# A decoder step on one Trainium2 core: the sample group's recurrence as wide vector work, a narrower weight load, and the closing halves swapped

## The chip, the core and the metric

The kernel runs on one core of a Trainium2 chip. TensorE multiplies matrices (its weight loads are listed apart, as PEld), VectorE (DVE) and ScalarE (ACT) work on 128 partitions side by side, GpSimd (POOL) makes masks and issues some transfers, and SyncE (SP) issues nearly all DMA transfers. Each engine works through its own queue in order and waits on semaphores. Matmuls write to PSUM, the accumulator memory; everything else lives in SBUF. The metric is the device time of one execution in microseconds; lower is better.

## The reference, cut to what matters

One inference step of a two-layer decoder serves a prompt of 1024 tokens and a sample group of 8 single tokens with the same weights. Layer 0 mixes tokens with a gated linear recurrence (4 heads, a 128 x 128 state per head) beside attention into a memory; layer 1 uses stick-breaking attention. Each layer ends in a SwiGLU feed-forward block. All is float32.

```
def step(S, inp):                      # recurrence, chunk by chunk
    b = jnp.cumsum(fi, axis=2)
    o_inter = jnp.einsum('bhtk,bhkv->bhtv', qi * jnp.exp(b), S)
    att = jnp.einsum('bhtk,bhsk,bhtsk->bhts', qi, ki, dec)
    o = o_inter + jnp.einsum('bhts,bhsv->bhtv', att, vi)
    S_new = jnp.exp(b_last[:, :, 0, :, None]) * S + jnp.einsum(
        'bhsk,bhsv->bhkv', ki * jnp.exp(b_last - b), vi)
    return S_new, o
h = h + rmsnorm(mix, g[1])
h = h + rmsnorm(swiglu(rmsnorm(h, g[2]), w_gu[l], w_down[l]), g[3])
```

For a sample there is one token, so the recurrence is one update: with the forget factor f, key k, value v and query q of a head (vectors of 128), the state becomes S = f * S + k v^T (f and k along the rows), and the output is q^T S. There are 8 samples x 4 heads = 32 such states, 2 MB in all; they are read, updated, and written back as an output.

## The kernel before

**Tiles.** Activations lie with features on partitions and tokens along the free dimension. The prompt is cut into two groups of 512 tokens; group 1 carries the 8 samples as columns 512 to 519 (`G : G + NB`). A float32 operand is split into a float32r high part (a cast on ScalarE) and a low part (a subtraction on VectorE, `split_to`), and products are made of three float32r matmuls. Plain float32 matmuls appear in the trace as two records each. Weights come in tiles of 128 x 512 (`split_w`, lines 201 to 207): a load on SyncE's queue, a cast, a subtraction, then 12 or 24 matmuls on line 220.

**The order of the work.** Each part of the program is a generator. `weave` advances several of them in turn, in proportion to given weights, each up to its next `yield`; this gives the program order. A planner then lays out every engine's queue when the kernel is built: among the instructions that its model of times says are ready, the one earliest in program order goes first. On the chip each queue then runs in that order, whatever the real times are. Buffers come from pools with a fixed number of slots: 4 of the 128 x 1024 kind (`C`), 7 of 128 x 512 (`B`), 3 PSUM banks for small products (`S`).

**The sample group's recurrence** (`hgrn_sample`, lines 1088 to 1145) is woven with the output gate's projection, a part of group 0's feed-forward block and the forming of weight sums:

```
weave((a1.sample(), 6), (a1.gate(), 4), (f0.part(1), 9), (w0, 9))
```

Keys and values of the 8 samples are transposed to 8 rows (lines 1096, 1097). Per head, the 8 states are loaded as a 128 x 1024 tile (line 1110), each 128 columns one sample. VectorE places each sample's value row at its own 128 columns of an 8 x 1024 tile with zeros elsewhere (line 1113, the constant `bdm`), and multiplies the state by the forget factors (line 1117). Two matmuls with 8 rows of weights form the outer products k v^T (line 1122), which VectorE adds to the state (line 1123). For the output, queries are spread into a 128 x 8 x 8 selector form (line 1105), so that eight matmuls of 128 x 8 weights (line 1125) put each sample's q^T S on its own row of `po`. The state is stored (line 1128). After the four heads, `po` is copied out (line 1131), transposed back to feature columns (line 1134), normalised, and written over the sample columns of the tile `Ft`, from which `merge` (line 1264) later takes it.

The same selector constant exists in float32r as `selr` and is used by `sample_pv` (line 948): weights of 128 x 8 that are all ones in one column sum the 128 partitions of a product onto one row. `sample_scores` (lines 914 to 937) sends 8 rows through a small DRAM tensor and reads them back on all 128 partitions.

**The prompt's recurrence** (`hgrn_prompt`, lines 1147 to 1223) builds the 128 x 128 block of attention weights of each chunk in seven levels of doubling block size m = 1 to 64. At each level a matmul of all 128 keys of a chunk (the weights) with the 64 queries of the upper half-blocks (line 1174) gives products, of which a predicated copy on VectorE (line 1184) takes those that a mask allows. At the top level, m = 64, the allowed ones are exactly those of the first 64 keys.

**The closing rows** (`ffn_w.close`, lines 664 to 695, and `out_rows`, lines 741 to 793). The last part of the last feed-forward block of group 1 works on one half of the columns after the other: 256 prompt columns first, then 256 prompt columns and the 8 samples (264). The first pass also loads and splits the weights. Each half ends with transposes to token rows (line 753), sums of squares by matmuls against a column of ones (line 768), two ScalarE operations for the norm, two VectorE operations per block of rows (lines 782 and 785) and a store per block: two blocks in the first half, three in the second (the samples being the third).

Of the kernel before, what the change touches and what calls it, by code (L numbers as in the profile page):

```python
# [18 lines left out]
P = 128  # L19
# [4 lines left out]
def tile_decoder(  # L24
# [550 lines left out]
    class ffn_w:  # L575
# [88 lines left out]
        def close(self, f0, nf, mids):  # L664

            l = self.l
            ws = []
            for a in range(2):
                d = slice(2 * P * a, (2 * P, NG[1])[a])
                h = d.stop - d.start  # L670
                acc = small([P, h], tag="st", bufs=3)
                rows = out_rows(self, a)
                for m in range(ND):
                    if a == 0:
                        ws.append(split_w(w_down[l], f0, nf, m * P, self.spl4))
# [9 lines left out]
                    nc.vector.tensor_add(R, R, ps[:, :h])  # L685
# [400 lines left out]
            yield  # L1086

    def hgrn_sample(Ft, Kt, Qt, vs):
        HB = H * NB
        kc = small([P, HB], tag="ss")  # L1090
        for h in range(H):
            nc.vector.tensor_copy(kc[:, h * NB : (h + 1) * NB], Kt[h // 2][:, h % 2, G : G + NB])
        pk = S()
        pvv = S()
        for h in range(H):
            nc.tensor.transpose(pk[:NB, h * P : (h + 1) * P], kc[:, h * NB : (h + 1) * NB], ident)
            nc.tensor.transpose(pvv[:NB, h * P : (h + 1) * P], vs[:, h, :], ident)
        kT = B()
        nc.vector.tensor_copy(kT[:NB, :512], pk[:NB, :])
        vT = B()  # L1100
        nc.vector.tensor_copy(vT[:NB, :512], pvv[:NB, :])
        po = S()
        for h in range(H):
            qd = small([P, NB, NB], tag="qd", bufs=2)
            nc.vector.tensor_mul(
                qd, sel, Qt[h // 2][:, h % 2, G : G + NB].unsqueeze(2).to_broadcast([P, NB, NB])
            )
# [5 lines left out]
            nc.vector.tensor_mul(  # L1113
                vbv[:NB], vT[:NB, h * P : (h + 1) * P].unsqueeze(1).to_broadcast([NB, NB, P]),
                bdm.to_broadcast([NB, NB, P]),
            )
            nc.vector.tensor_mul(
                stv, stv, Ft[h // 2][:, h % 2, G : G + NB].unsqueeze(2).to_broadcast([P, NB, P])
            )
            for a in range(2):  # L1120
                ps = S()
                nc.tensor.matmul(ps, kT[:NB, h * P : (h + 1) * P], vb[:NB, a, :], start=True, stop=True)
                nc.vector.tensor_add(st[:, a, :], st[:, a, :], ps)
            for b in range(NB):
                nc.tensor.matmul(
                    po[:NB, h * P : (h + 1) * P], qd[:, b, :], stv[:, b, :], start=(b == 0), stop=(b == NB - 1)
                )
            nc.sync.dma_start(st_sample[0, :, h].rearrange("b k v -> k b v"), stv)
            yield
        ot = B()  # L1130
        nc.vector.tensor_copy(ot[:NB, :], po[:NB, :])
        pr = S()
        for h in range(H):
            nc.tensor.transpose(pr[:, h * NB : (h + 1) * NB], ot[:NB, h * P : (h + 1) * P], ident[:NB, :NB])
# [12 lines left out]
    def hgrn_prompt(g, Ft, Kt, Qt, Vt):  # L1147
# [15 lines left out]
        for lv in range(7):  # L1163
            m = 1 << lv
            nbg = G // (2 * m)
            for hp in range(2):
# [3 lines left out]
                for hh in range(2):  # L1170
                    for c in range(CH):
                        cs = slice(c * P, (c + 1) * P)
                        rhs = Q_[:, hh, cs].rearrange("p (b t m) -> p b t m", t=2, m=m)[:, :, 1, :]
                        nc.tensor.matmul(plv[:, hh, c, :], K_[:, hh, cs], rhs, start=True, stop=True)  # L1174
                for hh in range(2):
                    Qv = Q_[:, hh, :G].rearrange("p (b t m) -> p b t m", t=2, m=m)
                    Kv = K_[:, hh, :G].rearrange("p (b t m) -> p b t m", t=2, m=m)
# [282 lines left out]
    with tc.issue_after(made[0].ins):  # L1460
# [47 lines left out]
        for blk in range(2):  # L1508
# [11 lines left out]
        nc.gpsimd.affine_select(  # L1520
            bdm.rearrange("p b o -> p (b o)"), ones[:NB, :NB], pattern=[[-1, NB]], compare_op=ALU.is_equal,
            fill=0.0, base=0, channel_multiplier=1,
        )
    drain(head)
    a0 = mixer_a(0, x0)
    drain(a0.v(), a0.fq())
# [100 lines left out]
```

## Time and profile before

| what | us |
|---|---|
| median of 3 runs | 2471.2 |
| lowest and highest of the 3 runs | 2469.78, 2472.68 |
| the profiled execution's own time | 2472.22 |
| its span, first to last instruction of the program | 2470.5 |
| largest group: matmuls of line 220 on normed inputs, 6240 records | 1119.5 busy |
| line 1174, 448 matmul records | 53.2 busy |
| mean traffic of the DMA engines | 160 GB/s |

How to read the lines that follow: the page has one row per group of instructions, with line number in the kernel, engine, operation, tile written <- tiles read, shapes, count, busy time, mean of one in ns, then the idle time of the engine just before and what ended it. The busy time of TensorE is of pipelined matmuls whose durations overlap, so the cost of one in a dense run is better read from the chain of waits, where a piece is start, duration, what, and the number of instructions in it. The chain follows the work that ended last back to its releasers, so that a piece of it is time that set the end. Stretches are given from the start of the span.

### The profile page before, as it was taken

To read this page: it belongs to the slowest core of one execution; us is meant where nothing else is said; L and a number is where in the kernel's file an instruction comes from. 1 tells how busy PE (TensorE), PEld (TensorE's weight loads), DVE (VectorE), ACT (ScalarE), POOL (GpSimd) and SP (SyncE) were. 2 spreads that over 40 slices of the span, in tenths; PEclk is the share of its full clock that TensorE was granted. 3 is DMA by queue.
4 is the path that set the end of the run, shared out by engine and by line. 5 is a ranking of instruction groups with operands and counts; after the bars stand their busy time and mean duration, and the time that the engine had idled before them with its cause. 6 is when DMAs were issued, how large, how long until landed. Compare 5 with 4: busy or idle time off the path is not lost.

```text
span 2470.5 us, 42287 instructions
## 1 busy us (share of the span) xinstructions
PE 2436.5 (99%) x15971; PEld 2176.6 (88%) x15971; DVE 1639.5 (66%) x2988; ACT 1236.6 (50%) x2377; POOL 184.2 (7%) x316
## 2 busy tenths in 40 slices
PE   8999999999999999999999999999999999999998
PEld 6888888877879998899999989877777888999998
DVE  5767556754788685655756685778688466755666
ACT  5437544243445554555444554555554445664445
POOL 1000101100000000111200101212000100000000
PEclk9999999999999999999999999999999999999999
DMA  6354666546745437767666649754253573465542
GB/s 188 116 167 111 156 192 160 127 134 164 212 150 154 140 120 227 201 163 183 162 196 174 193 128 274 228 150 146 91 177 117 138 199 120 139 187 145 152 143 74
DMA packets 530503, 395.29 MB, mean 160 GB/s; under 512 B 21237, under 2 KB 468802, under 8 KB 530298
## 3 DMA queue, kind: packets, MB, share of 16 engines
q1 hardware_dynamic: 501114, 312.88, 42.4%
q0 software_dynamic: 29184, 79.70, 14.0%
q8 instruction: 126, 2.06, 0.3%
q14 instruction: 79, 0.65, 0.1%
HBM read 362.69 MB, written 101.11 MB: 188 GB/s over the span
## 4 chain that ended last, share of the span: by engine, by line
PE 88%; DVE 5%; DMA 3%; issue 2%; ACT 2%; POOL 0%; SPq 0%; DVEq 0%; ACTq 0%; POOLq 0%
PE mm L220 47%; PE q L511 13%; PE q L648 9%; PE q L464 3%; PE s L1174 2%; PE mm L1042 2%; PE s L906 1%; DMA c<-in_cache_mem_v 1%; PE s L1370 1%; PE mm L824 1%; PE mm L851 1%; PE q L680 1%; PE s L875 1%; PE s L1336 1%; PE s L899 1%
## 5 line engine op out<-in xcount | busy, mean ns | idle before, releaser
L220 PE MATMUL mm<-x,ws 128*128 128x260 f32 (+1 forms) x6240 | 1119.5, 335 | 3.2 <-DVE r L657 1.7
L220 PEld LDWEIGHTS mm<-x,ws 128*128 128x128 f32 x6240 | 941.6, 188 | 127.3 <-issue 2.7
L206 ACT CAST ws<-w 128x512 fp32r<-128x512 f32 (+1 forms) x652 | 382.8, 588 | 548.9 <-PE mm L220 396.9
L207 DVE TENSOR_TENSOR ws<-w,ws 128x512 fp32r<-128x512 f32 (+1 forms) x652 | 419.2, 648 | 253.5 <-ACT ws L206 243.5
L220 PE MATMUL mm<-m,ws 128*128 128x512 f32 (+1 forms) x1344 | 280.3, 360 | 0.5 <-DVE r L400 0.5
L220 PEld LDWEIGHTS mm<-m,ws 128*128 128x128 f32 x1344 | 218.0, 188 | 37.2 <-issue 1.0
L648 PE MATMUL q<-m,ws 128*128 128x260 f32 (+1 forms) x1824 | 221.7, 282 | 0.0
L648 PEld LDWEIGHTS q<-m,ws 128*128 128x128 f32 x1824 | 218.9, 188 | 1.1 <-DVE t L534 0.3
L502 DVE TENSOR_TENSOR ws<-w,ws 128x512 fp32r<-128x512 f32 x181 | 123.9, 690 | 87.6 <-ACT ws L501 86.1
L501 ACT CAST ws<-w 128x512 fp32r<-128x512 f32 x181 | 111.8, 621 | 109.2 <-PE q L648 32.5
L511 PE MATMUL q<-x,ws 128*128 128x260 f32 (+1 forms) x1188 | 158.1, 282 | 0.0
L511 PEld LDWEIGHTS q<-x,ws 128*128 128x128 f32 x1188 | 148.6, 188 | 0.0
L511 PE MATMUL q<-y,ws 128*128 128x260 f32 x912 | 119.9, 283 | 0.4 <-ACT q L521 0.2
L511 PEld LDWEIGHTS q<-y,ws 128*128 128x128 f32 x912 | 113.7, 189 | 1.1 <-ACT q L518 0.6
L464 PE MATMUL q<-x,ws 128*128 128x260 f32 (+1 forms) x720 | 91.3, 284 | 0.3 <-DVE r L400 0.2
L464 PEld LDWEIGHTS q<-x,ws 128*128 128x128 f32 x720 | 88.4, 188 | 1.8 <-DVE r L400 0.5
L511 PE MATMUL q<-a,ws 128*128 128x260 f32 (+1 forms) x672 | 87.1, 282 | 0.0
L511 PEld LDWEIGHTS q<-a,ws 128*128 128x128 f32 x672 | 83.2, 188 | 0.0
L657 DVE TENSOR_TENSOR r<-r,q 128x260 f32<-128x260 f32 (+1 forms) x128 | 48.4, 420 | 48.8 <-PE q L648 48.8
L237 DVE TENSOR_SCALAR t<-mm 128x512 f32<-128x512 f32 (+1 forms) x58 | 40.1, 691 | 54.1 <-PE mm L220 53.8
L563 POOL COPY mk<-a 128x1 f32<-128x1 f32 x36 | 21.0, 583 | 645.6 <-ACT a L1226 393.9
L228 DVE TENSOR_TENSOR m<-t,m 128x512 fp32r<-128x512 f32 (+1 forms) x88 | 60.8, 691 | 9.5 <-ACT m L227 8.7
(358 smaller groups left out, 3038.2 us busy)
## 6 DMA issues: line engine op xcount, KB each, us to landing
w<-in_w_gu SPq DMA_DIRECT2D x297, 256.0 KB, 3.4
w<-in_w_down SPq DMA_DIRECT2D x160, 256.0 KB, 2.8
wsum<-in_w_gu POOLq DMA_DIRECT2D x72, 512.0 KB, 6.5
w<-wsum SPq DMA_DIRECT2D x104, 256.0 KB, 3.5
w<-in_w_in_a SPq DMA_DIRECT2D x80, 256.0 KB, 3.3
w<-in_w_o SPq DMA_DIRECT2D x64, 256.0 KB, 2.8
wsum<-in_w_gu POOLq DMA_DIRECT2D x24, 640.0 KB, 7.0
wsum<-wsum POOLq DMA_DIRECT2D x24, 512.0 KB, 5.8
```

Of the source, the lines that this page charges most:

```text
L206: nc.scalar.copy(ws[:, 0, :n, :], raw[:, :n, :])
L207: nc.vector.tensor_sub(ws[:, 1, :n, :], raw[:, :n, :], ws[:, 0, :n, :].bitcast(F32))
L220: nc.tensor.matmul(ps[:, a, : PW[g]], wt, xt[k][:, xi, o : o + PW[g]], start=(k == 0 and wi == 0), stop=(k == nk - 1 and wi == 2),)
L228: nc.vector.tensor_sub(dst[1], src, dst[0].bitcast(F32))
L464: ins = nc.tensor.matmul(pp[a][:, :h], wt, xt[k][:, xi, a * h : (a + 1) * h], start=(k == 0 and wi == 0), stop=(k == ND - 1 and wi == 2),)
L501: nc.scalar.copy(w[:, 0, :], src)
L502: nc.vector.tensor_sub(w[:, 1, :], src, w[:, 0, :].bitcast(F32))
L511: nc.tensor.matmul(ps[:, :h], w[:, wj, k * P : (k + 1) * P], x[:, xi, :], start=(first and k == 0 and wi == 0), stop=(k == 3 and wi == 2), ...
L648: nc.tensor.matmul(pp[a][:, :h], wt, mids[k][:, xi, a * h : (a + 1) * h], start=(k == 0 and wi == 0), stop=(k == nf - 1 and wi == 2),)
L657: nc.vector.tensor_add(d, d, pp[a][:, :h])
L1042: nc.tensor.matmul(pb[i][:, a, :], xt[k][:, xi, c * P : (c + 1) * P], ws[:, s, :], start=(k == 0 and wi == 0), stop=(k == ND - 1 and wi == 2),
L1174: nc.tensor.matmul(plv[:, hh, c, :], K_[:, hh, cs], rhs, start=True, stop=True)
```

## The change

Three edits.

1. In `hgrn_sample` the outer products and the output sums leave TensorE. The values of the 8 samples are written as 8 rows to a DRAM tensor (`vd`), and per head read back broadcast on all 128 partitions as a 128 x 1024 tile, as wide as the states. VectorE then makes f * S, k * v, their sum and q * S, each one operation of 1024 elements per partition. The last product is split in two float32r parts per half (512 columns, four samples), and matmuls with `selr` sum the partitions: row 2 h + a of `po` receives half a of head h, with four samples side by side. At the end the 8 rows go through a second DRAM tensor (`od`) to be regrouped from (head, half) rows to sample rows. There is one more `yield`, after the values' write. The key transposes, the selector form of the queries, and the constant `bdm` go.
2. In `close` the half with the samples comes first, and the weights are loaded with it.
3. In `hgrn_prompt`, at the top level, the matmul takes the first 64 keys alone as weights, and a plain copy on ScalarE of 64 partitions takes the place of the predicated copy.

```
-            for a in range(2):
+            for a in (1, 0):
...
-                    if a == 0:
+                    if a:
                         ws.append(split_w(w_down[l], f0, nf, m * P, self.spl4))
...
     def hgrn_sample(Ft, Kt, Qt, vs):
-        HB = H * NB
-        kc = small([P, HB], tag="ss")
-        for h in range(H):
-            nc.vector.tensor_copy(kc[:, h * NB : (h + 1) * NB], Kt[h // 2][:, h % 2, G : G + NB])
-        pk = S()
         pvv = S()
         for h in range(H):
-            nc.tensor.transpose(pk[:NB, h * P : (h + 1) * P], kc[:, h * NB : (h + 1) * NB], ident)
             nc.tensor.transpose(pvv[:NB, h * P : (h + 1) * P], vs[:, h, :], ident)
-        kT = B()
-        nc.vector.tensor_copy(kT[:NB, :512], pk[:NB, :])
         vT = B()
         nc.vector.tensor_copy(vT[:NB, :512], pvv[:NB, :])
+        vd = tc.dram_tile([NB, 512], F32, name=nm("vd"))
+        nc.sync.dma_start(vd, vT[:NB, :])
+        yield
...
         po = S()
         for h in range(H):
-            qd = small([P, NB, NB], tag="qd", bufs=2)
-            nc.vector.tensor_mul(
-                qd, sel, Qt[h // 2][:, h % 2, G : G + NB].unsqueeze(2).to_broadcast([P, NB, NB])
-            )
+            def col(t):
+                return t[h // 2][:, h % 2, G : G + NB].unsqueeze(2).to_broadcast([P, NB, P])
...
             nc.sync.dma_start(stv, state_hgrn[0, :, h].rearrange("b k v -> k b v"))
             vb = C()
             vbv = vb.rearrange("p a (b v) -> p (a b) v", v=P)
-            nc.vector.tensor_mul(
-                vbv[:NB], vT[:NB, h * P : (h + 1) * P].unsqueeze(1).to_broadcast([NB, NB, P]),
-                bdm.to_broadcast([NB, NB, P]),
-            )
-            nc.vector.tensor_mul(
-                stv, stv, Ft[h // 2][:, h % 2, G : G + NB].unsqueeze(2).to_broadcast([P, NB, P])
-            )
+            nc.sync.dma_start(vbv, vd[:, h * P : (h + 1) * P].partition_broadcast(P))
+            nc.vector.tensor_mul(stv, stv, col(Ft))
+            nc.vector.tensor_mul(vbv, vbv, col(Kt))
+            nc.vector.tensor_add(st, st, vb)
+            nc.sync.dma_start(st_sample[0, :, h].rearrange("b k v -> k b v"), stv)
+            nc.vector.tensor_mul(vbv, stv, col(Qt))
             for a in range(2):
-                ps = S()
-                nc.tensor.matmul(ps, kT[:NB, h * P : (h + 1) * P], vb[:NB, a, :], start=True, stop=True)
-                nc.vector.tensor_add(st[:, a, :], st[:, a, :], ps)
-            for b in range(NB):
-                nc.tensor.matmul(
-                    po[:NB, h * P : (h + 1) * P], qd[:, b, :], stv[:, b, :], start=(b == 0), stop=(b == NB - 1)
-                )
-            nc.sync.dma_start(st_sample[0, :, h].rearrange("b k v -> k b v"), stv)
-            yield
+                qs = B(F32R), B(F32R)
+                split_to(qs, vb[:, a, :])
+                for i, p in enumerate(qs):
+                    nc.tensor.matmul(
+                        po[:NB, :], selr[:, 2 * h + a, :], p,
+                        start=(h == 0 and a == 0 and i == 0), stop=(h == H - 1 and a == 1 and i == 1),
+                    )
+            yield
+        rows = B()
+        nc.vector.tensor_copy(rows[:NB, :], po[:NB, :])
+        od = tc.dram_tile([H, NB, P], F32, name=nm("od"))
+        nc.sync.dma_start(od.rearrange("h (a b) v -> (h a) b v", a=2), rows[:NB, :].rearrange("p (b v) -> p b v", v=P))
         ot = B()
-        nc.vector.tensor_copy(ot[:NB, :], po[:NB, :])
+        nc.sync.dma_start(ot[:NB, :].rearrange("p (h v) -> p h v", v=P), od.rearrange("h b v -> b h v"))
...
-                        nc.tensor.matmul(plv[:, hh, c, :], K_[:, hh, cs], rhs, start=True, stop=True)
+                        k = m if nbg == CH else P
+                        nc.tensor.matmul(
+                            plv[:k, hh, c, :], K_[:, hh, c * P : c * P + k], rhs, start=True, stop=True
+                        )
...
+                    if nb == 1:
+                        nc.scalar.copy(
+                            atts[hp * 2 + hh].rearrange("p (c t m) -> p c t m", c=CH, t=2)[:m, :, 1, :],
+                            plv[:m, hh, :, :],
+                        )
+                        continue
                     nc.vector.copy_predicated(
...
-        bdm = const.tile([NB, NB, 1], F32, name="bdm")
```

More of the change, by code (lines that the diff above doesn't have):

```diff
@@ L1088, in hgrn_sample @@
     def hgrn_sample(Ft, Kt, Qt, vs):
-        HB = H * NB
-        kc = small([P, HB], tag="ss")
-        for h in range(H):
-            nc.vector.tensor_copy(kc[:, h * NB : (h + 1) * NB], Kt[h // 2][:, h % 2, G : G + NB])
-        pk = S()
         pvv = S()
         for h in range(H):
-            nc.tensor.transpose(pk[:NB, h * P : (h + 1) * P], kc[:, h * NB : (h + 1) * NB], ident)
             nc.tensor.transpose(pvv[:NB, h * P : (h + 1) * P], vs[:, h, :], ident)
-        kT = B()
-        nc.vector.tensor_copy(kT[:NB, :512], pk[:NB, :])
         vT = B()
         nc.vector.tensor_copy(vT[:NB, :512], pvv[:NB, :])
+        vd = tc.dram_tile([NB, 512], F32, name=nm("vd"))
+        nc.sync.dma_start(vd, vT[:NB, :])
+        yield
+        HB = H * NB
+        assert 2 * H == NB
         po = S()
         for h in range(H):
-            qd = small([P, NB, NB], tag="qd", bufs=2)
-            nc.vector.tensor_mul(
-                qd, sel, Qt[h // 2][:, h % 2, G : G + NB].unsqueeze(2).to_broadcast([P, NB, NB])
-            )
+            def col(t):
+                return t[h // 2][:, h % 2, G : G + NB].unsqueeze(2).to_broadcast([P, NB, P])
             st = C()
@@ L1517, in tile_decoder @@
         nc.gpsimd.tensor_tensor(pidx, pidx, iot, op=ALU.add)
-        bdm = const.tile([NB, NB, 1], F32, name="bdm")
[L1520 to L1523, printed above, removed]
     drain(head)
```

## The prediction

> **What bounds the kernel now.** I read the page's busy shares first, then the chain of waits, then the chain and the timeline around the sample group's recurrence.
>
> ```profile
> span 2470.5 us, 42287 instructions
> PE 2436.5 (99%) x15971; PEld 2176.6 (88%) x15971; DVE 1639.5 (66%) x2988; ACT 1236.6 (50%) x2377; POOL 184.2 (7%) x316
> PE 88%; DVE 5%; DMA 3%; issue 2%; ACT 2%; POOL 0%; SPq 0%; DVEq 0%; ACTq 0%; POOLq 0%
> ```
>
> TensorE is busy 99% of the span and makes 88% of the chain that ends last. VectorE and ScalarE have slack on average. So the first question for each edit is how many microseconds of TensorE it removes in a stretch where TensorE has no gap, and the second whether it makes TensorE's queue wait.
>
> The edit's main place is the recurrence of the sample group. The chain between 480 and 640 us, in order of time (start, duration, what, count of matmul records), with its shares by line first:
>
> ```profile
> by line: PE mm L220 76.0%; PE s L1125 5.3%; PE s L1122 4.8%; PE s L1174 3.3%; PE s L1201 2.5%; PE s L1213 2.3%; PE s L1209 2.2%; PE s L256 1.9%; PE s L1195 1.1%; PE s L1096 0.3%; PE s L1097 0.3%; PE s L1134 0.2%; issue 0.0%
> 484.12 5.30 PE s L1174 x48
> ...
> 524.81 0.44 PE s L1096 x4
> ...
> 530.29 1.91 PE s L1122 x4
> ...
> 532.63 1.73 PE s L1125 x8
> 534.36 1.94 PE mm L220 x4
> 536.30 0.97 PE s L1125 x8
> 537.27 17.09 PE mm L220 x73
> 554.36 1.91 PE s L1122 x4
> ...
> 575.65 1.91 PE s L1122 x4
> ...
> 578.23 1.84 PE s L1125 x16
> ...
> 607.10 12.04 PE mm L220 x71
> ```
>
> The chain is TensorE from end to end: nothing but matmuls, back to back. Whatever leaves this queue here shortens the chain one for one, as long as nothing else takes its place. The recurrence's own shares are 4.8% of 160 us for line 1122 (four pieces of 1.91, 7.6 us), 5.3% for line 1125 (8.4 us) and 0.44 us for the key transposes of line 1096.
>
> The next rows are busy times by stretch (PE, weight loads, VectorE, ScalarE, GpSimd, then granted clock, DMA share, GB/s).
>
> ```profile
> 532.60:536.10 3.50, 3.50 (x13) 2.01 (x12) 2.32 (x3) 0.00 (x0) 0.00 (x0) 0.51 0.82 229
> sum 116.00, PE 115.98 PEld 89.67 DVE 66.67 ACT 46.30 POOL 8.09; mean PE 23.20 PEld 17.93 DVE 13.33 ACT 9.26 POOL 1.62
> ```
>
> The sum covers 524 to 640: TensorE 115.98 of 116 us, VectorE only 66.67, ScalarE 46.30. In the first row the clock is granted at 0.51 although TensorE is busy for all 3.50 us, right behind the first eight-row matmuls.
>
> **The change, part by part.** *Sample recurrence, TensorE.* It loses lines 1096, 1122 and 1125: 0.44 + 7.6 + 8.4 = 16.5 us. It gains 16 selector matmuls (4 heads, 2 halves, 2 split parts) of 8-column weights against 512 float32r columns. A 512-column record costs 17.09 / 73 = 0.234 us in the chain, so 16 cost 3.7 us; the same form exists on line 948, whose waits are small, and I add 0.3 us for such waits:
>
> ```profile
> L948 PE MATMUL ns<-b,selr 128*8 128x512 f32 x48 | 19.5, 434 | 0.8 <-DVE b L228 0.5
> L1174 PEld LDWEIGHTS s<-a,a 128*128 128x128 f32 x448 | 53.4, 192 | 1.2
> L1125 PEld LDWEIGHTS s<-c,qd 128*8 128x8 f32 x64 | 5.4, 93 | 3.5 <-issue 1.9
> ```
>
> Net -12.5 us. The value transposes (line 1097) and the output transposes (line 1134) stay.
>
> *The half clock.* The four line-220 records at 534.36 took 1.94 us where 4 x 0.234 = 0.94 would do. The dip follows matmuls that use 8 of 128 rows; they go, and -1.0 us with them. Line 948's 8-column form, which comes instead, ran at full clock (the row for 720 to 740, under rival B). Bounds: 0 if the dip comes from something else, -1.0 if not; I take -1.0, because it stands in this very stretch. The Trainium skill (TensorE: Matmul & The Clock Gate, What's actually happening) halves the clock after an idle window of about 3.4 us. This trace differs on the cause: TensorE was busy for all of those 3.50 us; by the page the dip would have nothing to do with these shapes and the sum would be 1.0 us less of a gain.
>
> *VectorE and ScalarE in that stage.* Rows of 524 to 640 (mean ns second from the bar):
>
> ```profile
> L207 DVE TENSOR_TENSOR ws<-w,ws 128x512 fp32r<-128x512 f32 x30 | 20.6, 688 | 8.4 <-ACT ws L206 8.4
> L1123 DVE TENSOR_TENSOR c<-c,s 128x512 f32<-128x512 f32 x8 | 5.4, 680 | 0.2 <-PE s L1122 0.2
> L1113 DVE TENSOR_TENSOR c<-b,bdm 8x1024 f32<-8x1024 f32 x4 | 4.8, 1210 | 0.6 <-DMA out_st_sample<-c 0.6
> L1117 DVE TENSOR_TENSOR c<-c,a 128x1024 f32<-128x1024 f32 x3 | 3.6, 1217 | 1.9 <-DMA c<-in_state_hgrn 1.9
> L1105 DVE TENSOR_TENSOR qd<-sel,a 128x64 f32<-128x64 f32 x2 | 0.4, 224 | 4.4 <-PE s L1125 4.4
> ACT ws L206 <- PE mm L220: 61.0, 26, 8.1
> ```
>
> Per head VectorE loses 0.22 + 1.21 + 2 x 0.68 = 2.8 us and gains three 1024-wide operations (key, add, query) and two split subtractions: 3 x 1.21 + 2 x 0.69 = 5.0 us. Over four heads that is +8.9 us, less one 0.68 us copy of the keys and four short ones. VectorE would be busy about 75 of 103 us; the cover is its idle time, so I cost it at 0. If that cover were gone it would cost up to 8.9 us. ScalarE gains eight casts of about 0.6 us, on 46.30 of 116. The last row (waits in this stage) is why: weights wait for TensorE, 61.0 us over 26 times, not TensorE for weights.
>
> *SyncE's queue and the loads.* It gains seven issues: the values' write, four broadcast loads, the outputs' write and read-back. Each broadcast moves 512 KB in 512-byte pieces, like the state's load. The nearest rows (DMA issues with us to landing; then SyncE's issues in time):
>
> ```profile
> c<-in_state_hgrn SPq DMA_DIRECT2D x4, 512.0 KB, 5.4
> b<-qd SPq DMA_DIRECT2D x24, 256.0 KB, 3.7
> out_y_prompt<-yT SPq DMA_DIRECT2D x4, 512.0 KB, 2.6
> 577.60 1.03 SPq L965 DMA_DIRECT2D c<-in_cache_mem_k  x1
> ...
> 611.87 0.37 SPq L965 DMA_DIRECT2D c<-in_cache_mem_k  x1
> 648.39 0.30 SPq L926 DMA_DIRECT2D qd<-b  x1
> 650.11 2.10 SPq L932 DMA_DIRECT2D b<-qd  x4
> ```
>
> A write to DRAM and the load that reads it are 1.7 us apart (648.39 to 650.11): that long SyncE stands once for the values and once for the outputs, with the weight loads behind it. Weights run ahead of TensorE here, so 0. The broadcasts land after about 5.4 us. Heads are about 20 us apart on TensorE (530.29, 554.36, 575.65), because the other matmuls of the weave are first in order, so the loads are covered: 0 of a possible 5.4 us per head.
>
> *The outputs' trip through DRAM.* Between the last selector matmul and line 1134's transposes there are now a write (1.7 us) and a read (below 3.7 us). Those transposes stand in TensorE's in-order queue; line 220's matmuls behind them wait if the data is late. Before, where only a copy stood between, 12.04 us of line-220 matmuls were laid there (607.10). Bounds: 0 and 5.4 us; I take +0.5. Everything behind (the norm, the gate's product) has its consumer a stage later.
>
> *One more pause.* The recurrence now yields once more ahead of its first head, so each head stands one step of the weave later, and with it the release of its two large buffers; the four memory-key loads at 577.60 to 611.87, which reuse them, move by up to 20 us. Their first use is after 650.11, and the last would land near 637: covered, 0.
>
> *The top level's 64 key columns.* 48 records of line 1174 take 5.30 us, 110 ns each, while the moving side has only 64 columns: the weight load paces them. A load of 128 columns shows 192 ns, one of 8 columns 93, so 0.83 ns per column, and 64 columns fewer save 53 ns. The level has 448 / 7 = 64 records. Bounds: 0 if 64 columns load no faster, 53 ns or 3.4 us at best. Where the load no longer paces, the moving side does: line 1125's records with 128 moving columns take 0.97 / 8 = 121 ns, so 64 may need some 60, which is 50 ns saved. I take that, the nearer end: -3.2 us. Eight predicated copies move from VectorE to plain copies on ScalarE; both have room, 0.
>
> *The closing order.* The work is the same; only the half behind the last matmul differs. Timeline of before, half 0 and then half 1:
>
> ```profile
> 2445.79 0.42 DVE L685 TENSOR_TENSOR r<-r,q 128x256 f32<-128x256 f32 x1
> ...
> 2450.47 0.74 DVE L785 SCALAR_TENSOR_TENSOR yT<-s,rr,hT 128x512 f32<-128x512 f32 x1
> 2459.83 1.47 PE L753 MATMUL s<-ident,r 128*128 128x128 f32 x12
> 2460.03 0.43 DVE L685 TENSOR_TENSOR r<-r,q 128x264 f32<-128x264 f32 x1
> 2466.45 0.73 DVE L785 SCALAR_TENSOR_TENSOR yT<-s,rr,c 8x512 f32<-8x512 f32 x1
> ```
>
> From the last addition to the last output operation half 0 takes 2451.21 - 2445.79 = 5.4 us, half 1 7.15: -1.7. But half 1's extra eight transposes (about 0.11 us each: 12 in 1.47) and four short sums now stand before the last matmul, about +1.2, and the store that lands last is 512 KB in place of 32 KB, perhaps +0.5. Sum 0, bounds -1.7 and +1.7.
>
> Sum: -12.5 - 1.0 + 0.5 - 3.2 + 0 = -16.2 us. The profiled execution took 2472.2 us (span 2470.5), 1.0 above the median of 2471.2; so 2456.0 there and 2455 for the median. A difference under 0.2% (4.9 us) is about what runs of this kernel cannot tell from none.
>
> **The rivals.** *A, full gain*: 2455. For it: no gap in TensorE over 116 us. Its own range is 2451 to 2461 (the top level saves nothing: +3.2; the trip costs 3 more; the tail's 1.7 each way).
>
> *B, the gain meets a full VectorE.* Later buffers push the sample group's memory attention, and with it VectorE work, into the stretch where VectorE has no room:
>
> ```profile
> 720.00:740.00 20.00, 19.21 (x110) 15.09 (x109) 18.68 (x33) 8.84 (x22) 0.00 (x0) 1.00 0.60 183
> sum 60.00, PE 58.50 PEld 48.14 DVE 54.82 ACT 31.62 POOL 0.76; mean PE 19.50 PEld 16.05 DVE 18.27 ACT 10.54 POOL 0.25
> ```
>
> From 700 to 760 VectorE works 54.82 of 60 us and TensorE already misses 1.5. About 8 us of added VectorE work there would be given back: 2463. Against it: the new work belongs 60 us earlier.
>
> *C, the trip stops TensorE.* If nothing is laid between, it stands 1.7 + 3.7 = 5.4 us, and a half-clock stretch like that of 532.60 costs 1.75 more: 7.2 in place of 0.5, 2462. Against: the 12 us laid between before. The Trainium skill (TensorE: Matmul & The Clock Gate, Why this matters for your kernels) warns of gaps over about 3 us between bursts of matmuls and so speaks for the second part; no such gap stands in the rows above.
>
> *D, the time was not TensorE's*: what supplies it sets the pace, and it idles for what it saved; 2471. Against: the 61.0 us of ScalarE waiting for TensorE.
>
> *E, slower: the heads' first selector matmul waits for its broadcast.* TensorE runs in order, so a late load stops it whole. At the full 5.4 us landing for each of four heads it loses 21.6 against a gain of 16.2: 2477. It decides from 16.2 / 4 = 4.05 us per head on. For: line 1117 once waited 1.9 us for a state. Against: 20 us between heads.
>
> **How the numbers follow.** A 0.62, B 0.13, C 0.08, D 0.06, E 0.11. Prediction: A's 2455. A, B and C are faster: 0.83; D is the same, 0.06; E slower, 0.11. The range runs over A, B and C: from 2449 (both best bounds and some luck in the order) to 2468.
>
> **What would show it.** Right: chain pieces of the recurrence of about 0.23 us per selector record and no lines 1122 and 1125; no clock of 0.5 near 535; level-six records at 60 ns; transposes of the outputs without a wait of TensorE ahead of them; TensorE's busy time lower by some 15 us. Wrong: a wait of TensorE on VectorE's split or on a broadcast at the selector matmuls (E), on the read-back (C), more than 1.5 us of TensorE gaps in the memory-attention stretch (B), or an order laid out anew that loses elsewhere.

## The result and the profile after

The changed kernel takes 2456.18 us in the median of four runs (2454.92 to 2457.05), the kernel before 2471.94 beside it (four runs, 2469.78 to 2473.18). The ratio is 0.9937, with an interval of 0.9920 to 0.9954. The profiled execution of the changed kernel took 2454.92 us, that of before 2472.22.

The page of the changed kernel (span, busy times by engine, shares of the chain):

```profile
span 2453.2 us, 42169 instructions
PE 2419.1 (99%) x15903; PEld 2167.8 (88%) x15903; DVE 1642.2 (67%) x2979; ACT 1241.7 (51%) x2393; POOL 184.3 (8%) x315
PE 88%; DVE 5%; DMA 3%; ACT 2%; issue 2%; POOL 0%; SPq 0%; DVEq 0%; ACTq 0%; POOLq 0%
```

TensorE is busy 17.4 us less (2436.5 to 2419.1) and the span is 17.3 us shorter. The shares of the chain stand as before: it is still a kernel bound by TensorE, with less for TensorE to do. VectorE's sum rose by 2.7 us over the whole span (1639.5 to 1642.2).

The chain of the changed kernel between 480 and 640 us (start, duration, what, count):

```profile
by line: PE mm L220 84.5%; PE s L1208 2.5%; PE s L1173 2.3%; PE s L1119 2.3%; PE s L1220 2.3%; PE s L1216 2.2%; PE s L256 1.9%; PE s L1202 1.1%; PE s L922 0.3%; PE s L1091 0.3%; PE s L1132 0.2%; issue 0.0%
...
482.94 3.74 PE s L1173 x48
...
522.22 0.44 PE s L1091 x4
522.65 0.29 PE s L256
522.95 22.33 PE mm L220 x97
545.27 0.93 PE s L1119 x4
546.20 16.84 PE mm L220 x96
563.04 0.92 PE s L1119 x4
...
586.15 0.92 PE s L1119 x4
587.07 12.69 PE mm L220 x78
599.76 0.92 PE s L1119 x4
600.68 19.62 PE mm L220 x108
620.30 0.34 PE s L1132 x4
```

The recurrence is now four pieces of 0.92 to 0.93 us (line 1119, the selector matmuls: 0.23 us per record, 3.7 us in all) between long pieces of line 220. The output transposes (line 1132) follow 19.62 us of line 220 without a gap. The 48 level records (line 1173, formerly 1174), 32 of the top level and 16 of the one below, take 3.74 us where 5.30 stood.

Busy times by stretch of the changed kernel (TensorE, weight loads, VectorE, ScalarE, GpSimd, clock, DMA share, GB/s), and the rows of the new forms by group (out<-in, shapes, count, busy, mean ns, idle before):

```profile
524.00:622.00 98.00, 98.00 (x496) 81.17 (x496) 66.08 (x100) 45.32 (x83) 10.15 (x16) 1.00 0.74 203
```

```profile
L1173 PEld LDWEIGHTS s<-a,a 128*128 128x128 f32 x384 | 45.9, 192 | 1.1
L1173 PEld LDWEIGHTS s<-a,a 128*64 128x64 f32 x64 | 4.0, 138 | 0.8 <-issue 0.7
L1119 PE MATMUL s<-b,selr 128*8 128x512 f32 x16 | 4.3, 392 | 0.0
```

TensorE is busy for all 98 us at a clock of 1.00; VectorE for 66.08. A weight load of 64 columns shows 138 ns against 192 for 128. The selector matmuls have 0.0 us of idle time ahead of them.

The end of the changed kernel (timeline; idle time and its releaser in brackets where there is any):

```profile
2443.66 0.42 DVE L685 TENSOR_TENSOR r<-r,q 128x256 f32<-128x256 f32 x1
...
2447.02 0.74 DVE L785 SCALAR_TENSOR_TENSOR yT<-s,rr,hT 128x512 f32<-128x512 f32 x1
2448.34 0.74 DVE L785 SCALAR_TENSOR_TENSOR yT<-s,rr,hT 128x512 f32<-128x512 f32 x1
```

From the last addition to the last output operation there are now 5.4 us (2443.66 to 2449.08), before 7.15.

**Where the time went.** The first matmul of the closing part starts 17.7 us earlier (2433.82 to 2416.16), and the end comes 17.3 us earlier (2470.51 to 2453.21): everything was gained ahead of the closing part, and 0.4 us was given back in it. The 17.7 us are 12.8 of the recurrence (16.5 removed, 3.7 added), 2.6 of the top level (1.56 in the chain of group 1; in group 0 the stage from the first record of line 824 to the last of line 851 went from 69.7 to 68.7 us) and 1.0 of line 220's records in the stretch at half clock that is gone. The other 0.8 of that stretch is in the 16.5 already: eight records of line 1125 took 1.73 us in it, where eight others take 0.97. Some 1.3 us are not assigned.

### The profile page after: what moved, and what is told of

It reads as the page before. It is cut to its first block, busy times and chain, and to the rows that moved or that the text cites. A ratio compares the mean times of both kernels' runs of the same rounds, so it can differ in the third digit from the quotient of the medians.

```text
span 2453.2 us, 42169 instructions
## 1 busy us (share of the span) xinstructions
PE 2419.1 (99%) x15903; PEld 2167.8 (88%) x15903; DVE 1642.2 (67%) x2979; ACT 1241.7 (51%) x2393; POOL 184.3 (8%) x315
## 4 chain that ended last, share of the span: by engine, by line
PE 88%; DVE 5%; DMA 3%; ACT 2%; issue 2%; POOL 0%; SPq 0%; DVEq 0%; ACTq 0%; POOLq 0%
PE mm L220 47%; PE q L511 13%; PE q L648 9%; PE q L464 4%; PE s L1173 2%; PE mm L1042 2%; PE s L906 1%; PE s L1377 1%; PE mm L824 1%; PE s L875 1%; PE mm L851 1%; PE q L680 1%; PE s L1343 1%; PE s L899 1%; DMA c<-in_cache_mem_v 1%
## 5 line engine op out<-in xcount | busy, mean ns | idle before, releaser
L566 POOL DMA_DIRECT2D wsum<-in_w_gu x64 | 58.5, 931 | 116.2 <-DMA wsum<-wsum 101.8
```

The costliest lines, as they stand in the source:

```text
L566: nc.gpsimd.dma_start(d, a, accum_op=ALU.add)
```

## The experiments

All ratios are to the kernel before as it ran beside each experiment; its median there went from 2471.9 to 2475.2, so differences of a few us between medians of different experiments say little by themselves. My theory was the forecast's: TensorE's queue has no gap, so each matmul record that leaves it is gained one for one, whatever the data's new path costs elsewhere. Rivals were a cost hidden in the new path (the trip through DRAM, VectorE, the broadcasts) and a gain from the half clock and not from the records.

**The recurrence alone.** The other two edits undone:

```
-            for a in (1, 0):
+            for a in range(2):
...
-                        nc.tensor.matmul(
-                            plv[:k, hh, c, :], K_[:, hh, c * P : c * P + k], rhs, start=True, stop=True
-                        )
+                        nc.tensor.matmul(plv[:, hh, c, :], K_[:, hh, cs], rhs, start=True, stop=True)
```

> The recurrence edit alone. Theory (TensorE is the bound, and the time it no longer spends is the gain): 16.5 us of matmuls and 1.0 us of half clock go, about 4 us of selector matmuls come, so 13 us less than before, near 2459. Rival (the order laid out anew brings or takes several us by itself, so that the edits do not add up): anything from 2452 to 2468.

Measured: 2457.8 us (six runs, 2454.78 to 2461.46), ratio 0.9931 (0.9914 to 0.9949). By the medians, 15.0 us (2472.8 for the kernel before): nearly the whole of the change. The runs lie in two groups, three from 2454.8 to 2455.6 and three from 2460.0 to 2461.5; what may part them is told under "What the hardware showed".

**The top level alone**; the plain copy of 64 partitions goes with it.

```
-                        nc.tensor.matmul(plv[:, hh, c, :], K_[:, hh, cs], rhs, start=True, stop=True)
+                        k = m if nbg == CH else P
+                        nc.tensor.matmul(
+                            plv[:k, hh, c, :], K_[:, hh, c * P : c * P + k], rhs, start=True, stop=True
+                        )
```

> The 64 key columns at the top level alone. Theory (the weight load paces these records, about 50 ns saved on each of 64): 3.2 us less than before, near 2468.7, and records of the top level about 60 ns apart. Rival (a load of 64 columns costs what 128 cost): the same as before, 2472, records still 110 ns apart.

Measured: 2473.74 us (12 runs, 2467.87 to 2477.09), ratio 1.0001 (0.9990 to 1.0011). No gain shows in the times. The chain of this run has the shorter piece all the same, and its stretches say where it went:

```profile
484.17 3.74 PE s L1175 x48
```

```profile
532.30:535.70 3.40, 3.40 (x12) 1.84 (x12) 1.25 (x2) 0.00 (x0) 0.00 (x0) 0.50 0.98 286
556.20:559.60 3.40, 3.40 (x14) 1.46 (x12) 0.00 (x0) 0.00 (x0) 0.00 (x0) 0.50 0.95 247
```

Two stretches of 3.4 us at half clock stand in the old recurrence, where before's profile has one. The second took back about 1.7 of some 2.6 us in this execution, whose span is 2470.0 against 2470.5. Whether that holds for the other eleven runs can't be seen; the size, about 0.1%, is within their scatter of 9 us. The mechanism is shown, the gain in time is not.

**The closing order alone.**

```
-            for a in range(2):
+            for a in (1, 0):
...
-                    if a == 0:
+                    if a:
```

> The closing order alone. Theory (1.7 us less behind the last addition, 1.2 us of transposes moved ahead of it, a larger last store): the same as before within 1 us, 2472. Rival (the shorter last half is a gain outright): 1.7 us less, 2470. Second rival (the larger last store decides): 1 us or more slower.

Measured: 2472.34 us (12 runs, 2469.64 to 2482.64), ratio 0.9995 (0.9982 to 1.0009): no difference. From the start of the closing part to the end there are 37.15 us, 36.7 before. A stretch of its recurrence, the same code as before's:

```profile
532.30:536.00 3.70, 3.70 (x22) 2.13 (x21) 3.02 (x4) 0.00 (x0) 0.00 (x0) 1.00 0.75 211
```

The clock is 1.00 where before's profile had 0.51 at the same instructions: the dip that I had booked does not come in every execution.

**The change without the closing order.** The edit is the last diff turned round, on the changed kernel.

> The changed kernel with the closing order of before. Theory (the closing order is worth nothing): the changed kernel's time, 2456 within 1 us. Rival (it gives 1.7 us): 2458. Second rival (it takes 1 us): 2455.

Measured: 2458.64 us (six runs, 2453.83 to 2460.97), ratio 0.9931 (0.9914 to 0.9947), against 0.9937 for the whole change. With the run above: the closing order is worth nothing that can be measured.

**Outer products back on TensorE**, the queries' half left as changed:

```
-            nc.sync.dma_start(vbv, vd[:, h * P : (h + 1) * P].partition_broadcast(P))
+            nc.vector.tensor_mul(
+                vbv[:NB], vT[:NB, h * P : (h + 1) * P].unsqueeze(1).to_broadcast([NB, NB, P]),
+                bdm.to_broadcast([NB, NB, P]),
+            )
...
-            nc.vector.tensor_mul(vbv, vbv, col(Kt))
-            nc.vector.tensor_add(st, st, vb)
+            for a in range(2):
+                ps = S()
+                nc.tensor.matmul(ps, kT[:NB, h * P : (h + 1) * P], vb[:NB, a, :], start=True, stop=True)
+                nc.vector.tensor_add(st[:, a, :], st[:, a, :], ps)
```

> The changed kernel with the outer products back on TensorE (eight-row weights, key transposes, masked values), the output sums still by selectors. Theory: the 7.6 + 0.44 us of those matmuls come back, about 2464; and if the half clock of before comes from matmuls with eight rows, it may stand near them again, 1 us more. Rival (the half clock came from the eight-column query matmuls, or from nothing in this code): no clock of 0.5 in mid-span.

**Queries back on TensorE**, the outer products left as changed:

```
-            nc.vector.tensor_mul(vbv, stv, col(Qt))
-            for a in range(2):
-                qs = B(F32R), B(F32R)
...
+            for b in range(NB):
+                nc.tensor.matmul(
+                    po[:NB, h * P : (h + 1) * P], qd[:, b, :], stv[:, b, :], start=(b == 0), stop=(b == NB - 1)
+                )
...
-        nc.sync.dma_start(ot[:NB, :].rearrange("p (h v) -> p h v", v=P), od.rearrange("h b v -> b h v"))
+        nc.vector.tensor_copy(ot[:NB, :], po[:NB, :])
```

> The changed kernel with the output sums back on the 128 x 8 query matmuls, the outer products still on VectorE, no second trip through DRAM. Theory: 7.0 to 8.4 us of those matmuls come back, 4 us of selector matmuls and the trip's 0.5 go, so about 2460, and the clock stays at full. Rival (the eight-column weights make the half clock): a clock of 0.5 near them.

Measured: 2463.49 us with the outer products back (five runs, 2462.63 to 2469.91; ratio 0.9962, 0.9948 to 0.9976) and 2461.41 with the queries back (four runs, 2460.86 to 2465.43; 0.9956, 0.9940 to 0.9973). By the medians they cost 7.3 and 5.2 us over the changed kernel. The records that came back, a piece in the chain of the one and of the other (4 records of outer products, and 16 of queries, are one head):

```profile
546.66 1.91 PE s L1121 x4
```

```profile
591.47 1.84 PE s L1119 x16
```

Four pieces of 1.91 and the 0.44 of key transposes make 8.1 against 7.3 measured. The query records take some 7.4 us at full clock (1.84 for each head's 16), so with the 3.7 of selectors gone they explain 3.7 of the 5.2. The rest has a row of its own in that run; behind it stand VectorE's wait for the broadcasts and two pieces of the chain:

```profile
PE mm L220 <- DVE t L716: 1.7, 2, 1.2
DVE c L1115: 11.7, 3
543.27 9.20 DMA c<-vd
556.51 8.13 DMA c<-vd
```

VectorE works in order too. While it stands 11.7 us in three waits for late broadcasts, a product of the feed-forward block (line 716) waits behind them in its queue, and TensorE waits 1.7 us in all for that product. Neither the kernel before nor the changed kernel has this wait. Together the halves come to 12.5 us by the runs and 11.8 by the records, with the 1.7 of waits beside. So the records are paid, and neither half alone makes the gain; but in this order of the work the broadcasts were not covered. The intervals of the three kernels overlap at their ends, so it is the sizes in the traces, not the runs by themselves, that carry this.

**Two more trips through DRAM** behind the outputs' write:

```
+        for _ in range(2):
+            hop = B()
+            nc.sync.dma_start(hop[:NB, :].rearrange("p (h v) -> p h v", v=P), od.rearrange("h b v -> b h v"))
+            od = tc.dram_tile([H, NB, P], F32, name=nm("od"))
+            nc.sync.dma_start(od.rearrange("h b v -> b h v"), hop[:NB, :].rearrange("p (h v) -> p h v", v=P))
```

> The changed kernel with two more read-and-write rounds in the outputs' trip through DRAM, four more transfers one behind the other. Theory (the transposes behind it are laid later in TensorE's order, behind other matmuls): 2456 within 1 us, the transposes about 8 us later. Rival (TensorE stands for the trip): 4 transfers of at least 1.7 us, 7 us or more slower, 2463 or more, with a wait of TensorE ahead of the transposes.

Measured: 2459.66 us (four runs, 2454.05 to 2461.88), ratio 0.9948 (0.9932 to 0.9965), which overlaps the changed kernel's interval. The timeline of its profiled execution (2454.05 us) shows why (first write, last read, first transpose that uses it):

```profile
602.58 0.30 SPq L1127 DMA_DIRECT2D od<-b  x1
...
615.62 0.29 SPq L1134 DMA_DIRECT2D b<-od  x1
...
621.03 0.41 PE L1137 MATMUL s<-ident,b 8*128 8x8 f32 x4
```

Three trips instead of one fit between the last selector matmul and the transposes: the last read is issued 13.0 us after the first write, the transposes come 5.4 us later, line 220 runs all the while, and TensorE waits for nothing there. The transposes stand where the changed kernel has them (620.30), not 8 us later as I had expected: they had that much room. One trip therefore costs 0. The three timed runs from 2459.6 on are like the upper group of the first experiment; the profile of one execution can't say what they waited for.

**More work for VectorE.** The product with the queries is made three times per head (eight operations more; the result is the same):

```
             nc.vector.tensor_mul(vbv, stv, col(Qt))
+            nc.vector.tensor_mul(vbv, stv, col(Qt))
+            nc.vector.tensor_mul(vbv, stv, col(Qt))
```

> The changed kernel with the query product made three times over in each head: eight more VectorE operations of 1.21 us, 9.7 us. Theory (VectorE's idle time covers it): 2456 within 1 us. Rival (the gain already meets a full VectorE): up to 9.7 us slower, 2466.

Measured: 2457.3 us (four runs, 2455.01 to 2459.91), ratio 0.9933 (0.9916 to 0.9949), as the changed kernel. The same stretch:

```profile
524.00:622.00 98.00, 98.00 (x498) 81.12 (x497) 74.40 (x106) 45.34 (x81) 20.48 (x14) 1.00 0.73 202
```

VectorE is busy 8.3 us longer (66.08 to 74.40) and TensorE still for all 98.00. VectorE's cover in this stage is real, with 24 us to spare even then.

**No pause ahead of the first head:**

```
         nc.sync.dma_start(vd, vT[:NB, :])
-        yield
```

> The changed kernel without the added pause ahead of the first head. Theory (the later release of buffers is covered): 2456 within 1 us. Rival (later buffers push the memory attention's VectorE work into a full stretch): up to 3 us less than the changed kernel, 2453.

Measured: 2461.16 us (five runs, 2459.29 to 2464.73), ratio 0.9945 (0.9931 to 0.9959). By the medians 5 us more; but the kernel before beside it was at 2475.15, and by the ratios it is 2.0 us, with overlapping intervals. The timeline of its first selector matmul, and the stretch behind it:

```profile
539.28 0.40 PE L1118 MATMUL s<-b,selr 128*8 128x512 f32 x1 [2.12 <-ACT b L227]
```

```profile
540.10:543.50 3.40, 3.40 (x10) 2.03 (x9) 3.40 (x6) 1.64 (x4) 0.91 (x2) 0.51 0.73 210
```

Without the pause TensorE stands 2.12 us in front of the first head's sums and then runs 3.4 us at half clock. Their data came late because VectorE had stood 1.64 us for the first broadcast and then 0.47 us for the state's load, issued right behind it. In the changed kernel the same matmul comes at 545.27 with no wait. So the pause that I had costed at 0 for the buffers behind it is what covers the first head's trip.

**Level five narrowed as well.** At m = 32 each of the two allowed 32 x 32 blocks gets a matmul of its own, with 32 keys as weights and 32 queries moving, and plain copies of 32 partitions take the predicated copy's place:

```
-                        k = m if nbg == CH else P
...
+                        if m < 32:
+                            nc.tensor.matmul(plv[:, hh, c, :], K_[:, hh, cs], rhs, start=True, stop=True)
+                            continue
+                        for b in range(64 // m):
+                            o = 2 * b * m
+                            nc.tensor.matmul(
+                                plv[o : o + m, hh, c, b * m : (b + 1) * m], K_[:, hh, c * P + o : c * P + o + m],
+                                Q_[:, hh, c * P + o + m : c * P + o + 2 * m], start=True, stop=True,
+                            )
```

> The changed kernel with the level below the top (m = 32) also narrowed: each of its matmuls of 128 keys is replaced by two of 32 keys and 32 queries that write their own quarter of the partitions, and the predicated copy by two plain copies. Theory (records are paced by the columns loaded, so 32 columns take some 35 to 45 ns each): 4 records of 40 in place of 2 of 110, 64 ns saved per replaced matmul, 32 of them, 2 us less than the changed kernel, 2454. Rival (about 60 ns is the least that a record costs): 4 x 60 in place of 220, 0.6 us more, 2457.

Measured: 2449.73 us (five runs, 2449.26 to 2457.54), ratio 0.9907 (0.9890 to 0.9923). Its chain, first in group 1 and then in group 0, and the row of the new weight loads:

```profile
480.94 2.67 PE s L1177 x64
...
147.91 0.63 PE s L1177 x32
...
151.50 1.07 PE s L1177 x16
```

```profile
L1177 PEld LDWEIGHTS s<-a,a 128*32 128x32 f32 x128 | 2.5, 112 | 1.1 <-issue 0.5 <-PE mm L220 0.4
```

The first piece mixes both narrowed levels, 32 records of 32 columns and 32 of 64. The second holds 32 records of 32 columns alone and the third 16 of 64: 0.63 / 32 = 20 ns and 1.07 / 16 = 67 ns each. So a record of 32 columns takes about half of the 35 to 45 ns of my theory, and the rival's 60 ns is out. For the whole level 128 such records take 2.5 us where 64 of 110 ns took 7.0: 4.5 us less. The median is 6.4 us below the changed kernel's (7.4 by the ratios), and the intervals meet. It has the lowest median of all kernels run here; its lead over the changed kernel is 4.5 us by its records and not settled by the times.

**The first key load emitted ahead of group 1's heads**, once on the changed kernel and once on that with level five narrowed (why is told under "What the hardware showed"):

```
+    ready = []
+
+    def head_kv(g, h):
+        kh, vh = A(), A()
...
-            kh, vh = A(), A()
-            nc.sync.dma_start(kh[:, : g + 1, :G], ksc[h][:, : g + 1, :])
-            nc.sync.dma_start(vh[:, : g + 1, :G], vsc[h][:, : g + 1, :])
+            kh, vh = ready.pop() if ready else head_kv(g, h)
...
+    ready.append(head_kv(1, 0))
```

> The changed kernel with one move: the first head's keys and values of group 1's stick-breaking attention are loaded ahead of its query projection, some tens of microseconds earlier. In the profiles so far TensorE waits 0 to 5.0 us for this load, and where it waits 2.5 us or more, 3.4 or 6.8 us at half clock follow. Theory (this wait and its half clock make the scatter between executions): no wait of TensorE on this load, no half clock near 1570, executions all near the lowest of the changed kernel, 2453 to 2456. Rival (the scatter comes from elsewhere): executions spread over 2454 to 2461 as before.

> The same move in the kernel with the level below the top narrowed as well (4 matmuls of 32 keys by 32 queries). Theory: the gains add, 2449 or less with little scatter. Rival (the order laid out anew takes it back): 2454.

Measured: 2454.71 us (six runs, 2452.63 to 2455.51; ratio 0.9924, 0.9911 to 0.9936) and 2452.74 us (five runs, 2450.61 to 2453.56; 0.9914, 0.9901 to 0.9928). Neither profile has a wait for that load, though in neither does the load leave SyncE earlier (1556.63 and 1555.29, against 1555.33 in the changed kernel). Both kernels beat the kernel before; against the changed kernel the medians are 1.5 and 3.4 us lower with overlapping intervals, and the second is not below the 2449.73 of level five alone. Each run lies within 3 us of its kernel's fastest.

## Why the prediction was right, step by step

2455 was forecast, 2456.2 measured, and rival A, the full gain, is what happened. TensorE had no gap, 68 of its records went, and its busy time and the span fell by the same 17 us. That the median came within 1.2 us is in part luck: the top level gave 0.6 less than booked, the trip cost 0.5 less and the closing order 0.4 more, 1.3 us came that no term accounts for, and single executions of one kernel lie several us apart.

- *Recurrence, TensorE: right.* -12.5 us was forecast, and the records of before's profile give -12.8: the selectors take 3.7 us as booked, and the 0.3 us booked for their waits did not come (0.0 in their row). Without the half clock, which is in 0.8 of it, it would be -12.0.
- *The half clock: booked as a fixed term, and it is not one.* The dip at 532.6 is absent in the run of the closing order, which leaves the recurrence as it was, and comes twice in that of the top level. In those three profiles it followed 3 of the 12 heads of the old recurrence. Where it came in before's profile it cost 1.0 us in four records of line 220, as booked, and some 0.8 in line 1125's, which the 8.4 us of the forecast held already. The changed kernel's profile did not show it, but with either half of the old matmuls alone it did not come either, in eight heads. That the two kinds together bring it about is a guess; it stays open. The Trainium skill (TensorE: Matmul & The Clock Gate, What's actually happening) ties a halved clock to a window of idle time. What counts for that is the time ahead of the stretch, not the stretch itself, by which the forecast argued. Ahead of the two stretches at 532.30 and 556.20 TensorE was busy for 4.30 of 4.30 and 20.20 of 20.20 us (528.00 to 532.30, 536.00 to 556.20), so the trace does not agree here.
- *VectorE and ScalarE costed at nothing: right.* 66.08 of 98 us was busy, 67%, where I had put 75 of 103, 73%; 8.3 us more changed nothing.
- *SyncE and the loads: right in cost for this kernel, wrong in size.* I had 5.4 us for a broadcast to land. In the run with the queries on TensorE it was 9.2, the one landing that its trace has (DMA issues, last number), and in the changed kernel VectorE waited twice, 4.1 us in all; the first wait (timeline):

```profile
c<-vd SPq DMA_DIRECT2D x4, 512.0 KB, 9.2
```

```profile
532.14 1.23 DVE L1111 TENSOR_TENSOR c<-c,a 128x1024 f32<-128x1024 f32 x1 [2.13 <-DMA c<-vd]
```

  That load was issued at 525.36, so it took up to 6.8 us. The other matmuls laid ahead covered it: 22.33 us of line 220, and then the first selector matmul at 545.27 with nothing idle ahead of it. The heads' selectors stand 13.6 to 23.1 us apart, not always 20. That the cover is the order's and not certain shows where the queries stayed on TensorE: there late broadcasts cost TensorE 1.7 us, by way of VectorE's queue, a path that the forecast did not have.
- *The trip through DRAM: 0, not +0.5.* Three trips fit.
- *One more pause: its sign was missed.* I looked only at what it delays and found nothing, which holds. What it gives, cover for the first head, I did not see; without it rival E's wait is there, 2.1 us for one head.
- *The top level: right by the records.* 62 ns for each (1.98 us for 32 of the 48 records in the chain, the other 16 at 110) against 60 forecast, and 138 ns for the load where 192 - 53 = 139 was forecast. The times alone do not show this part, and group 0's stage gained 1.0 us, not 1.6.
- *The closing order: 0 forecast, +0.4 measured*, 36.7 to 37.05 us from the start of the closing part. The terms: -1.7 between the last addition and the last output operation, as forecast; +1.3 for what moved ahead of it (forecast 1.2); +0.8 from the last output operation to the end (forecast 0.5; 3.3 us became 4.1). In the runs it can't be seen.
- *The rivals.* B: the memory attention gave nothing back; the whole 17.7 us arrive at the closing part. C falls with the three trips. D falls with the two halves, which cost what their records take or more. E's wait at the selectors came only without the pause, and at 2.1 us once it is far from 4.05 us per head.

## What to carry to other kernels

Where TensorE's queue has no gaps, read a record's cost from its spacing in the chain (0.23 us for 512 columns; 110, 62 and 20 ns for weights of 128, 64 and 32 columns here; a piece of the chain can mix shapes), and count what leaves: work moved to an engine that is busy two thirds of the stage came at no charge here. Then look for cover: the longer way of the data costs nothing as long as an in-order TensorE has enough other matmuls laid ahead of its use, and a single pause in the program order can be what provides it. The engine that takes the work has its own order: where it stood for a late load, what TensorE needed from it came late as well. A gain of 0.1% must be read from the records, because the runs do not resolve it.

## What the hardware showed that I had not expected

**A short wait of TensorE costs more than itself.** At the start of group 1's stick-breaking attention the first matmul uses a key tile that is loaded just before. The rows of TensorE's waits for that load (us, times, longest), in the changed kernel, the recurrence alone, the change without the closing order, that without the pause, that with more VectorE work, and that with the outer products on TensorE:

```profile
PE s L1343 <- DMA a<-ksc: 1.2, 1, 1.2
```

```profile
PE s L1334 <- DMA a<-ksc: 2.6, 1, 2.6
```

```profile
PE s L1343 <- DMA a<-ksc: 4.4, 1, 4.4
```

```profile
PE s L1342 <- DMA a<-ksc: 5.0, 1, 5.0
```

```profile
PE s L1345 <- DMA a<-ksc: 4.2, 1, 4.2
```

```profile
PE s L1353 <- DMA a<-ksc: 2.5, 1, 2.5
```

In the five executions with a wait of 2.5 us or more a stretch of 3.4 or 6.8 us at half clock came at its end; in the others, with 1.2 us or less, none did there. The stretch of the change without the closing order:

```profile
1566.40:1573.20 6.80, 5.20 (x14) 3.65 (x15) 2.91 (x7) 1.26 (x2) 0.00 (x0) 0.50 0.88 298
```

TensorE worked 5.20 of those 6.80 us at a clock of 0.50; the wait ran into the stretch's first 1.6 us. By an estimate from these figures the half clock cost 5.2 / 2 = 2.6 us on top of the 4.4. The Trainium skill (TensorE: Matmul & The Clock Gate, Why this matters for your kernels) warns of gaps over about 3 us; here gaps of 2.1 and 2.5 us came with the half clock too, and one of 1.86 us in the change without the closing order (1476.6), while a gap of 2.1 us in the run with three trips did not. The profiled executions with the long wait took 2459.9 us and more, those of the changed kernel and of the run with three trips, without it, 2454 to 2455: the same 5 us that part the two groups of the recurrence's runs. That every timed run of the upper group had this wait is likely and not shown, since only one execution of each kernel has a profile. With the load emitted earlier, the wait was absent in both profiles and no run lay in an upper group. But the profile of the run with three trips lacks the wait as well, and in the traces of the edit the load left SyncE no earlier and TensorE still found it landed, so it is open whether the edit cured it or those runs were spared.

**Narrow float32 weights save more than their share.** Records with weights of 128, 64 and 32 columns (and 64, 64 and 32 columns moving) are 110, 62 and 20 ns apart, while their loads show 192, 138 and 112 ns. The loads shrink by 0.84 and 0.81 ns per column. The spacing follows that roughly from 128 to 64 columns and then falls below it: 32 columns at 0.8 ns would make some 26 ns, an estimate from the loads. In the records of 32 columns the starts come in pairs, 6 to 7 ns apart, with some 32 ns from one pair to the next. Each matmul there writes its own quarter of the partitions; whether that is what lets two run together was not tested. Two records of 32 columns (40 ns) beat one of 128 by more than my forecast of 35 to 45 ns for each had it.
